# ConvFFN of a diffusion backbone layer: where the up-projection gives back its lead of four pairs

## The chip, the cores and the metric

The kernel runs on one core of one Trainium2 chip. The metric is the device time of one execution, in microseconds; the median of three runs is compared.

## The reference

One layer over 1024 latent tokens of width 1024, with a context prefix of 256: modulated RMSNorm, an input projection that feeds an attention branch and a long-convolution branch, a merge, then a modulated RMSNorm and the ConvFFN, and a final RMSNorm. The change touches the ConvFFN alone:

```python
def dwconv3(u, w, b):
    up = jnp.pad(u, ((0, 0), (1, 1), (0, 0)))
    return up[:, :-2] * w[0] + up[:, 1:-1] * w[1] + up[:, 2:] * w[2] + b

def conv_ffn(h, w_up, b_up, conv_w, conv_b, w_down, b_down):
    u = dwconv3(h @ w_up + b_up, conv_w, conv_b)
    a, g = jnp.split(u, 2, axis=-1)
    return (jax.nn.gelu(a) * g) @ w_down + b_down
```

Here `h` is 1024 x 1024, `w_up` 1024 x 5632 (a and g of 2816 each) and `w_down` 2816 x 1024.

## The kernel before, in words

All products are fp32 in three matmuls (`mm3`, lines 184 to 186): each operand is split into a high part (a cast to fp32r on ScalarE) and a low part (a subtract on VectorE, line 174, "a low" below). High by high, high by low and low by high add up in PSUM.

**The up-projection** goes over 22 pairs j. A pair is 128 columns of a and the same 128 of g, for all 1024 tokens. It is a 2 x 2 block product (halves of the 1024 inputs by halves of the tokens) done with seven products of blocks instead of eight. Each product is 4 x 3 = 12 matmuls of 128 x 512. They are numbered 1 to 7; seq names them (p, j). Their moving operands, sums of the token blocks, stay in SBUF for all pairs: `B1` (tiles m0h and m0l) for 1 and 2, T2, T3, T4, T1 and B22 for 6, 7, 4, 5 and 3. Their weights are made for each pair: the loads of four blocks of `w_up` go into a ring of five `raw` buffers (line 1317), product 6 needs three sums on VectorE (wsum) and product 3 one, and each product one cast (whi) and one low (wlo).

Products 2, 4 and 3 add onto the banks of 1, 7 and 5 after VectorE or ScalarE has read those. In the order of a pair (`behind`, line 1592):

- behind 1: ScalarE copies the bank (c1); behind 6: VectorE's u2 = c1 + bank of 6, and ScalarE's copy ca LOW empties the bank of 1 and 2
- behind 7: VectorE's u3 = u2 + bank of 7; only then may 4 write that bank
- behind 5: cg HIGH = u3 + bank of 5; only then may 3 write that bank
- behind 4: cg LOW = u2 + bank of 7 and 4, then ScalarE's first convolution tap of g (conv ug, line 1556)
- behind 3: ca HIGH = u2 + bank of 5 and 3, then conv ua

Work that can wait goes on a list (`later`, `due`) and is issued one to three products further: VectorE's other two taps of g (taps ug) and of a (taps ua), ScalarE's gelu, VectorE's ug = ua x ug and the store to `act_d`.

**The order** is a list written out by hand (`seq`, lines 1460 to 1469), and the engines' order follows it (`manual_schedule`). Products 1 and 2 of a pair depend on nothing of that pair, so they run four pairs ahead (AHEAD) and stand between 7 and 5, and between 4 and 3, of an earlier pair. Pairs 18 to 21 have no further pair to take them from. In their place stand pieces of the down-projection's first product, (8, 0) to (8, 5), 48 matmuls in all, whose operands are eight blocks of `act_d` and `w_down`, cast and split into the tiles of B1, which are free by then.

While product n runs, `ahead(reach(n))` prepares the weights up to four products further (pieces (8, k) are not counted) and issues loads three products beyond that. In each step stand, in this order: the matmuls, the loads, sums and casts of the preparation, `behind`, the lows of the preparation, and `due`.

**The down-projection** follows: products (9, 4) and (9, 5) still with blocks in the old pools, then units of two blocks from line 1695 on (`fetch_unit`, `prepare_unit`), whose first buffers (ff, raw, rr, bh, bl, ah, al) take the memory of the pools of B1, B22, T1 and the weights.

PSUM holds four banks b1 (for 1 and 2, and for the down-projection's sums X) and four banks b (for 6, 7 and 5).

Of the kernel before, what the change touches and what calls it, by code (L numbers as in the profile page):

```python
# [24 lines left out]
NJ = DFF // P  # L25
# [140 lines left out]
def build(tc, A, out, stop=99):  # L166
# [6 lines left out]
    def sub(out, a, b, eng=V):  # L173
        eng.tensor_tensor(out=out, in0=a, in1=b, op=ALU.subtract)  # L174
# [33 lines left out]
    one = gp.tile([P, 1], F32, name="one")  # L208
# [1233 lines left out]
    def second_tiles(c, late):  # L1442
# [12 lines left out]
        for d, t_ in them:  # L1455
# [4 lines left out]
    AHEAD = 4  # L1460
    second = lambda c: ("T", c)
    seq = [(1, 0), (1, 1), (2, 0), second(0), (2, 1), second(1), (1, 2), second(2), (1, 3), second(3),
           (2, 2), (2, 3)]
    for j in range(NJ):
        more = j + AHEAD < NJ
        early = {18: [(), (8, 0), (8, 1)], 19: [(8, 2), (8, 3)], 20: [(8, 4)], 21: [(8, 5)]}.get(j, [])
        seq += [(6, j), (7, j)] + [(1, j + AHEAD)] * more + early[:1] + [(5, j), (4, j)] + [(2, j + AHEAD)] * more + early[1:] + [(3, j)]
    seq += [(9, 4), (9, 5)]
    seq = [s for s in seq if s]
    prods = [s for s in seq if s[0] != "T"]  # L1470
    raws, sums_, wts, early = {}, {}, {}, {}
    X = [None] * 4
# [8 lines left out]
    def prepare(p, j):  # L1481

        new = lambda: cpool.tile([P, 512], F32, name="wsum", tag="wsum", bufs=3)
        src = None
        if p >= 8:
            if p == 8 and j >= 4:
                return lambda: None
            if p == 8:

                parts_ = [[b_[:, 2 * j + n] for b_ in B1] for n in range(2)]  # L1490
            else:
                parts_ = [[wp.tile([P, 512], F32R, name=t_, tag=t_, bufs=6) for t_ in ("whi", "wlo")] for n in range(2)]
            early[j] = [*parts_[0], *parts_[1]]
            r_ = raws.pop((p, j))
            for d, src in zip(parts_, r_):
                S.copy(out=d[0], in_=src)

            def lows():
                for d, src in zip(parts_, r_):
                    sub(d[1], src, d[0])  # L1500
            return lows
        if p == 6:
            r21, r22, r11 = (raws[6, j, b_] for b_ in (A21, A22, A11))
            s1, s2, s3 = new(), new(), new()
            tt(s1, r21, r22, ALU.add)
            sub(s2, s1, r11)
            sub(s3, r11, r21)
            sums_[j] = s1, s2, s3
            src = s2
        elif p == 7:  # L1510
            src = sums_[j][2]
        elif p == 5:
            src = sums_[j][0]
        elif p == 4:
            src = raws.pop((6, j, A22))
        elif p == 3:
            src = new()
            sub(src, raws.pop((3, j, A12)), sums_.pop(j)[1])
        else:
            src = raws.pop((p, j, A11 if p == 1 else A12))  # L1520
        hi = wp.tile([P, 512], F32R, name="whi", tag="whi", bufs=6)
        S.copy(out=hi, in_=src)
        lo = wp.tile([P, 512], F32R, name="wlo", tag="wlo", bufs=6)
        wts[p, j] = hi, lo
        return lambda: sub(lo, src, hi)
# [45 lines left out]
    def product(p, j):  # L1571
        if p >= 8:
            for i, ks in {(8, 0): ((0, (0,)),), (8, 1): ((0, (1,)),), (8, 2): ((0, (2,)), (1, (0, 1, 2))),
                          (8, 3): ((0, (3,)), (1, (3,))), (8, 4): ((2, (0, 1, 2, 3)),),
                          (8, 5): ((3, (0, 1, 2, 3)),)}.get((p, j), [(i, (j,)) for i in range(4)]):
                for k in ks:
                    if k == 0:
                        X[i] = pa.tile([P, 512], F32, name="b1", tag="b1")
                    down_mm(X[i], i, k, early[k], k == 0, False)
            return  # L1580
        th, tl = {1: [b_[:, 0:4] for b_ in B1], 2: [b_[:, 4:8] for b_ in B1], 3: B22, 4: T4, 5: T1, 6: T2,
                  7: T3}[p]
        key = {2: 1, 4: 7, 3: 5}.get(p, p)
        if key == p:
            banks[key, j] = pa.tile([P, 512], F32, name="b1" if p == 1 else "b", tag="b1" if p == 1 else "b")
        ps = banks[key, j]
        wh, wl = wts.pop((p, j))
        for k in range(4):
            ks = slice(k * P, k * P + P)
            mm3(ps, wh[:, ks], wl[:, ks], th[:, k], tl[:, k], k == 0 and key == p, k == 3, key != p)  # L1590
# [55 lines left out]
    for s in seq:  # L1646
        if s[0] == "T":
            second_tiles(s[1], None)
            continue
        if s == (6, 0):  # L1650
            for pl in (tmp, hf0p, yp1):
                pl.release()
            fw_ = tc.alloc_tile_pool(name="fw_", bufs=1, reuse_waits="tile")
        product(*s)
        n_ += 1
        low = ahead(reach(n_))
        if s[0] == 9:
            continue
        if s == (3, NJ - 1):
            for k in (4, 5):  # L1660
                product(9, k)
        behind(*s)
        for f in low:
            f()
        if s == (3, NJ - 1):
            break
        due()
# [216 lines left out]
```

## Time and profile before

| what | value |
|---|---|
| median of three runs | 2041.69 us (2036.03 to 2044.32) |
| profiled execution: time / span | 2043.09 us / 2041.3 us |
| mean granted TensorE clock | 0.968 |
| busy TensorE / VectorE / ScalarE / GpSimd | 1897.0 / 1569.8 / 975.7 / 436.8 us |
| up-projection, first conv ug of a pair to the last | 1419.94 to 1825.08 us |
| regular pair, 1440 to 1747 us | one every 19.2 us |

The profile is of one execution. Times count from the first instruction. TensorE's weight loads (PEld) run beside its matmuls (PE). Every matmul of 128 x 512 is listed with 0.39 us, but one starts every 0.23 us, so busy times of matmuls overlap; starts are what counts. The value in brackets at a row's end is how long the engine was idle before it and what ended that. The granted clock is 1.00 at 2.4 GHz and 0.50 at 1.2. The program's names lose their numbers in the profile's rows: u2 and u3 are both u, m0h and m0l are B1.

### The profile page before, as it was taken

How to read it: one execution, taken by the hardware profiler on the slowest of the kernel's cores; microseconds unless marked ns; L12 is line 12 of the kernel's file. 1: busy time of each engine (PE TensorE's matmuls, PEld its weight loads, DVE VectorE, ACT ScalarE, POOL GpSimd, SP SyncE). 2: the span in 40 equal slices, each digit the busy share in tenths (PEclk: the TensorE clock that was granted, in tenths of full speed). 3: DMA queues.
4: the chain of work that ended last, by engine and by line, in shares of the span. 5: the costliest groups of instructions: out<-in, count | busy, mean ns of one | idle time of the engine just before them, and what ended most of it. 6: DMA issues, size and time to landing. Idle time of an engine off the chain costs nothing.

```text
span 2041.3 us, 27758 instructions
## 1 busy us (share of the span) xinstructions
PE 1897.0 (93%) x9776; PEld 1572.0 (77%) x9776; DVE 1569.8 (77%) x2634; ACT 975.7 (48%) x1966; POOL 436.8 (21%) x278
## 2 busy tenths in 40 slices
PE   6788899889998998999999999998999999899997
PEld 1576778779888987788888777777888888678885
DVE  6998887697887634577777664789888888878687
ACT  3574544343244345577777332245444444445443
POOL 3453323212122132254432132440000000000000
PEclk8799999999999999999999999999999999899999
DMA  7426523747555441345433884742333323349762
GB/s 258 162 91 206 161 96 126 245 133 249 194 171 154 129 147 57 123 126 161 150 99 49 289 289 138 262 165 73 119 97 115 119 94 118 119 141 346 243 206 100
DMA packets 181131, 322.54 MB, mean 158 GB/s; under 512 B 26955, under 2 KB 65359, under 8 KB 180096
## 3 DMA queue, kind: packets, MB, share of 16 engines
q1 hardware_dynamic: 156256, 287.01, 43.3%
q10 hardware_dynamic: 24736, 33.76, 4.7%
q8 instruction: 77, 1.26, 0.3%
q14 instruction: 62, 0.51, 0.1%
HBM read 245.03 MB, written 75.68 MB: 157 GB/s over the span
## 4 chain that ended last, share of the span: by engine, by line
PE 58%; DVE 23%; DMA 7%; issue 6%; ACT 3%; POOL 2%; SPq 0%; DVEq 0%; ACTq 0%; POOLq 0%
PE mm L185 6%; PE mm L186 6%; PE mm L184 6%; PE b L184 6%; PE b L185 6%; PE b L186 6%; PE tp L1154 3%; DMA wm<-w_mod 2%; PE s L185 2%; PE s L184 2%; PE s L186 2%; POOL wlo L174 2%; PE o L185 2%; PE o L186 2%; PE o L184 2%
## 5 line engine op out<-in xcount | busy, mean ns | idle before, releaser
L174 POOL TENSOR_TENSOR wlo<-raw,whi 128x512 fp32r<-128x512 f32 x138 | 232.5, 1696 | 550.7 <-ACT whi L500 401.5
L184 PE MATMUL mm<-hTh,whi 128*128 128x512 f32 x448 | 179.4, 401 | 1.4 <-ACT sg L983 1.4
L185 PE MATMUL mm<-hTl,whi 128*128 128x512 f32 x448 | 178.5, 399 | 0.7 <-DVE hTl L174 0.7
L186 PE MATMUL mm<-hTh,wlo 128*128 128x512 f32 x448 | 179.0, 399 | 0.0
L1056 DVE TENSOR_REDUCE mx<-s 128x1 f32<-128x512 f32 (+1 forms) x192 | 113.5, 599 | 59.7 <-PE s L186 58.2
L185 PE MATMUL mm<-wlo,hTh 128*128 128x256 f32 x416 | 119.7, 288 | 8.7 <-POOL wlo L174 8.4
L1061 ACT ACTIVATE Pt<-s,mx 128x512 f32<-128x512 f32 (+1 forms) x192 | 116.1, 614 | 20.5 <-DVE mx L1059 19.1
L184 PE MATMUL mm<-whi,hTh 128*128 128x256 f32 x416 | 119.4, 288 | 1.2 <-DVE hf L606 1.2
L186 PE MATMUL mm<-whi,hTl 128*128 128x256 f32 x416 | 119.6, 288 | 0.0
L388 ACT CAST Xh<-X 128x512 fp32r<-128x512 f32 x128 | 78.2, 621 | 86.1 <-DVE X L177 32.4
L174 DVE TENSOR_TENSOR PTl<-tp,PTh 128x512 fp32r<-128x512 f32 x160 | 108.5, 687 | 13.9 <-ACT PTh L1156 10.4
L1156 ACT CAST PTh<-tp 128x512 fp32r<-128x512 f32 x160 | 92.7, 594 | 41.0 <-PE tp L1154 40.6
L186 PE MATMUL b<-bh,al 128*128 128x512 f32 x284 | 110.7, 390 | 0.6 <-DVE al L174 0.6
L184 PE MATMUL b<-bh,ah 128*128 128x512 f32 x284 | 110.7, 390 | 0.5 <-ACT ah L1741 0.5
L185 PE MATMUL b<-bl,ah 128*128 128x512 f32 x284 | 110.6, 390 | 0.0
L500 ACT CAST whi<-raw 128x512 fp32r<-128x512 f32 x110 | 66.7, 618 | 87.8 <-PE mm L185 39.2
L174 DVE TENSOR_TENSOR Xl<-X,Xh 128x512 fp32r<-128x512 f32 x112 | 83.1, 760 | 31.0 <-ACT Xh L388 30.7
L184 PEld LDWEIGHTS mm<-hTh,whi 128*128 128x128 f32 x448 | 85.7, 191 | 16.7 <-ACT sg L983 1.8
L186 PEld LDWEIGHTS mm<-hTh,wlo 128*128 128x128 f32 x448 | 85.7, 191 | 15.8
L185 PEld LDWEIGHTS mm<-hTl,whi 128*128 128x128 f32 x448 | 85.5, 191 | 16.1 <-DVE hTl L174 1.1
L1154 PEld LDWEIGHTS tp<-ident,Pt 128*128 128x128 f32 x640 | 77.8, 141 | 22.9 <-issue 4.0
L1154 PE MATMUL tp<-ident,Pt 128*128 128x128 f32 x640 | 94.4, 274 | 1.0 <-DVE PTl L174 0.8
(396 smaller groups left out, 5833.9 us busy)
## 6 DMA issues: line engine op xcount, KB each, us to landing
raw<-w_up SPq DMA_DIRECT2D x132, 256.0 KB, 2.8
raw<-w_in SPq DMA_DIRECT2D x88, 256.0 KB, 3.3
wm<-w_mod SPq DMA_DIRECT2D x64, 256.0 KB, 4.1
raw<-act_d SPq DMA_DIRECT2D x25, 512.0 KB, 3.2
wd<-w_down SPq DMA_DIRECT2D x44, 256.0 KB, 3.9
ws_d<-wd SPq DMA_DIRECT2D x44, 256.0 KB, 4.5
act_d<-ug SPq DMA_DIRECT2D x44, 256.0 KB, 2.2
ft<-fwd_d SPq DMA_DIRECT2D x28, 384.0 KB, 4.0
```

Source lines behind the costliest of these rows:

```text
L174: eng.tensor_tensor(out=out, in0=a, in1=b, op=ALU.subtract)
L184: T.matmul(o, lh, rh, start=start, stop=False, skip_group_check=more)
L185: T.matmul(o, lh, rl, start=False, stop=False, skip_group_check=more)
L186: last_mm[0] = T.matmul(o, ll, rh, start=False, stop=stop, skip_group_check=more)
L388: S.copy(out=h, in_=X)
L500: S.copy(out=hi, in_=raw)
L1056: V.tensor_reduce(out=mx[:, j:j + 1], in_=s[:, :n], axis=AX.X, op=ALU.max)
L1061: S.activation(out=Pt[:, o:o + n], in_=sps[j][:, :n], func=AF.Exp, bias=mx[:, 3:4], accum_out=sm[:, j:j + 1])
L1154: T.transpose(tp[:, i * P:i * P + P], cur[i][:, kt * P:kt * P + P], ident)
L1156: S.copy(out=th, in_=tp)
```

## The change

Products 1 and 2 of the next pair are left out at three pairs on the way (6, 11 and 16), so the lead falls from four to three, two and one there, and pairs 18 to 20 have products 1 and 2 in their places like the others. All six pieces of the down-projection's first product move to the end: (8, 0) to (8, 3) between 4 and 3 of pair 21, (8, 4) and (8, 5) behind product (3, 21), ahead of (9, 4) and (9, 5). The lows of the early blocks are issued in the preparation, ahead of `behind`, and no longer after it.

```diff
@@ -1461,12 +1461,16 @@
     second = lambda c: ("T", c)
     seq = [(1, 0), (1, 1), (2, 0), second(0), (2, 1), second(1), (1, 2), second(2), (1, 3), second(3),
            (2, 2), (2, 3)]
+    nxt = AHEAD
     for j in range(NJ):
-        more = j + AHEAD < NJ
-        early = {18: [(), (8, 0), (8, 1)], 19: [(8, 2), (8, 3)], 20: [(8, 4)], 21: [(8, 5)]}.get(j, [])
-        seq += [(6, j), (7, j)] + [(1, j + AHEAD)] * more + early[:1] + [(5, j), (4, j)] + [(2, j + AHEAD)] * more + early[1:] + [(3, j)]
+        more = nxt < NJ and j not in (6, 11, 16)
+        one, two = [(1, nxt)] * more, [(2, nxt)] * more
+        nxt += more
+        if j == NJ - 1:
+            one, two = [], [(8, n) for n in range(4)]
+        seq += [(6, j), (7, j)] + one + [(5, j), (4, j)] + two + [(3, j)]
+    seq += [(8, 4), (8, 5)]
     seq += [(9, 4), (9, 5)]
-    seq = [s for s in seq if s]
     prods = [s for s in seq if s[0] != "T"]
@@ -1498,6 +1502,9 @@
             def lows():
                 for d, src in zip(parts_, r_):
                     sub(d[1], src, d[0])
+            if p == 8:
+                lows()
+                return lambda: None
             return lows
@@ -1657,8 +1664,8 @@
         if s[0] == 9:
             continue
         if s == (3, NJ - 1):
-            for k in (4, 5):
-                product(9, k)
+            for x_ in prods[n_:]:
+                product(*x_)
         behind(*s)
```

The order on VectorE in pair 6 before, from u2 (u_15618) over the taps ua of pair 5, u3 (u_15643) and two lows to ug of pair 5 and the sums for pair 7:

```order
L177 TENSOR_TENSOR u_15618<-c_15019,b 128x512
L174 TENSOR_TENSOR wlo<-raw,whi 128x512
L180 SCALAR_TENSOR_TENSOR ua<-ca,vecs,ua 128x1023 x2
L177 TENSOR_TENSOR ua<-ua,edge_ff 128x2
L177 TENSOR_TENSOR u_15643<-u_15618,b 128x512
L174 TENSOR_TENSOR wlo<-raw,whi 128x512
L174 TENSOR_TENSOR wsum<-raw,wsum 128x512
L174 TENSOR_TENSOR wlo<-wsum,whi 128x512
L177 TENSOR_TENSOR ug<-ua,ug 128x1024
L177 TENSOR_TENSOR wsum<-raw 128x512
L174 TENSOR_TENSOR wsum<-wsum,raw 128x512
L174 TENSOR_TENSOR wsum<-raw 128x512
```

The same stretch of VectorE now, from the sum for product 3 that stands ahead of u2 to cg HIGH (u3 is u_15649):

```order
L174 TENSOR_TENSOR wsum<-raw,wsum 128x512
L177 TENSOR_TENSOR u_15618<-c_15019,b 128x512
L174 TENSOR_TENSOR wlo<-wsum,whi 128x512
L180 SCALAR_TENSOR_TENSOR ua<-ca,vecs,ua 128x1023 x2
L177 TENSOR_TENSOR ua<-ua,edge_ff 128x2
L177 TENSOR_TENSOR wsum<-raw 128x512
L174 TENSOR_TENSOR wsum<-wsum,raw 128x512
L174 TENSOR_TENSOR wsum<-raw 128x512
L177 TENSOR_TENSOR u_15649<-u_15618,b 128x512
L174 TENSOR_TENSOR wlo<-wsum,whi 128x512
L177 TENSOR_TENSOR cg<-u_15649,b 128x512
```

The preparation counts in products and a bare pair has fewer of them, so the sums for the next pair stand ahead of u3 now and the sum for product 3 ahead of u2.

The order on VectorE at the start of pair 21 now, from ca HIGH of pair 20 to u3 (u_17991):

```order
L177 TENSOR_TENSOR ca<-u_17769,b 128x512
L174 TENSOR_TENSOR wlo<-raw,whi 128x512
L174 TENSOR_TENSOR m0l<-raw,m0h 128x512 x8
L174 TENSOR_TENSOR wsum<-raw,wsum 128x512
L177 TENSOR_TENSOR u_17959<-c_17816,b 128x512
L174 TENSOR_TENSOR wlo<-wsum,whi 128x512
L180 SCALAR_TENSOR_TENSOR ua<-ca,vecs,ua 128x1023 x2
L177 TENSOR_TENSOR ua<-ua,edge_ff 128x2
L177 TENSOR_TENSOR u_17991<-u_17959,b 128x512
```

All eight lows of the early blocks stand there in one piece, ahead of the sum for product 3 and of u2; before, they stood in pair 18 (four behind u2, two behind cg LOW) and pair 19 (two).

## Rows read from the trace of the kernel before

**Rows 1.** The stretch 1440 to 1747 (busy us and count by engine, clock, DMA).

```profile
core 0: us, PE busy (x) PEld busy (x) DVE busy (x) ACT busy (x) POOL busy (x), PEclk, DMA share, GB/s
1440.00:1747.00 307.00, 307.00 (x1349) 251.96 (x1348) 262.04 (x368) 134.73 (x192) 0.00 (x0) 1.00 0.34 110
```

**Rows 2.** Waits of VectorE and of TensorE's weight loads, 1440 to 1747 (total, times, longest).

```profile
DVE wlo L174 <- ACT whi L1522: 42.1, 48, 1.2
PEld b L184 <- ACT ca L1604: 3.0, 11, 0.3
```

**Rows 3.** Timeline of ScalarE: conv ug of pairs 16 and 17 (start, us, [idle before]).

```profile
1728.02 1.24 ACT L1556 ACTIVATE ug<-cg,cbias_ff,vecs 128x1024 f32<-128x1024 f32 x1 [1.18 <-DVE cg L177]
...
1747.22 1.25 ACT L1556 ACTIVATE ug<-cg,cbias_ff,vecs 128x1024 f32<-128x1024 f32 x1 [1.18 <-DVE cg L177]
```

**Rows 4.** Timeline of VectorE, pair 18 without the lead's products.

```profile
1752.32 0.68 DVE L177 TENSOR_TENSOR ca<-u,b 128x512 f32<-128x512 f32 x1
1752.92 0.68 DVE L174 TENSOR_TENSOR wlo<-raw,whi 128x512 fp32r<-128x512 f32 x1
1756.28 0.69 DVE L174 TENSOR_TENSOR wsum<-raw,wsum 128x512 f32<-128x512 f32 x1 [2.68 <-DMA raw<-w_up]
...
1757.49 2.49 DVE L174 TENSOR_TENSOR m0l<-raw,m0h 128x512 fp32r<-128x512 f32 x4
1759.90 0.69 DVE L174 TENSOR_TENSOR wlo<-wsum,whi 128x512 fp32r<-128x512 f32 x1
1760.50 2.60 DVE L180 SCALAR_TENSOR_TENSOR ua<-ca,vecs,ua 128x1023 f32<-128x1023 f32 x2
...
1765.15 0.68 DVE L177 TENSOR_TENSOR u<-u,b 128x512 f32<-128x512 f32 x1
...
1771.47 0.69 DVE L177 TENSOR_TENSOR cg<-u,b 128x512 f32<-128x512 f32 x1 [2.70 <-PE b L186]
```

**Rows 5.** Timeline of TensorE, pair 18; the last row is pair 21.

```profile
1757.85 0.39 PE L186 MATMUL b<-m1l,wlo 128*128 128x512 f32 x1
1765.97 0.77 PE L184 MATMUL b<-T4h,whi 128*128 128x512 f32 x1 [7.73 <-DVE u L177]
...
1772.30 0.40 PE L184 MATMUL b<-m0h 128*128 128x512 f32 x1
...
1815.84 0.50 PE L184 MATMUL b<-m0h 128*128 128x512 f32 x1 [0.45 <-ACT ca L1604]
```

**Rows 6.** Timeline of ScalarE: casts of four early blocks, pair 18.

```profile
1754.25 2.17 ACT L1496 CAST m0h<-raw 128x512 fp32r<-128x512 f32 x4
```

**Rows 7.** Timeline of TensorE: three other idles of some 3 us.

```profile
537.03 0.58 PE L184 MATMUL zp<-Xh,ft 128*128 128x256 f32 x1 [3.10 <-ACT Xh L388]
...
834.77 0.50 PE L184 MATMUL o<-PTh,v 128*128 128x512 f32 x1 [2.74 <-ACT PTh L1156]
...
1302.49 0.39 PE L1202 MATMUL tr<-ah,ones 128*1 128x512 f32 x1 [3.10 <-ACT ah L1198]
```

**Rows 8.** Windows behind those idles, columns as in rows 1.

```profile
537.00:541.00 4.00, 3.97 (x18) 3.97 (x19) 3.21 (x8) 1.14 (x2) 2.76 (x1) 0.50 0.01 2
836.50:840.50 4.00, 4.00 (x16) 3.29 (x15) 1.86 (x3) 1.47 (x4) 0.19 (x1) 0.57 0.98 345
1302.50:1306.50 4.00, 3.78 (x16) 2.81 (x17) 4.00 (x4) 0.62 (x1) 2.27 (x2) 1.00 0.92 294
```

**Rows 9.** Timeline of SP's queue, ScalarE and TensorE: the down-projection starts.

```profile
1822.59 0.40 SPq L1695 DMA_DIRECT2D ff<-act_d  x1
1827.07 0.38 SPq L1695 DMA_DIRECT2D ff<-w_down  x1
...
1830.93 1.05 ACT L1740 CAST bh<-ff 128x1024 fp32r<-128x1024 f32 x1 [1.83 <-DMA ff<-w_down]
...
1832.98 0.50 PE L184 MATMUL b<-bh,ah 128*128 128x512 f32 x1 [0.50 <-ACT ah L1741]
```

**Rows 10.** Tile raw, 1745 to 1775: its loads from issue to landing.

```profile
DMA to landing us min/median/max: 2.7/2.9/3.1
```

## The prediction

> **What bounds the kernel now.** I read four views of the up-projection stage, in this order. First the busy table of the regular stretch, pairs 2 to 17: TensorE is busy 307.00 of 307 us, VectorE 262.04 [rows 1]. That alone says TensorE is the limit. Second, who waits for whom there: VectorE's only wait is for ScalarE's casts, 42.1 us in 48 waits, and the only one on TensorE's side is 3.0 us in 11 weight loads, for ScalarE's copy that empties a bank [rows 2]; ScalarE's waits are all for VectorE. Neither of the two waits for TensorE. Third, the period: one pair takes 1747.22 - 1728.02 = 19.20 us [rows 3]. VectorE's work is 262.04 / 16 pairs = 16.4 us and its waits 42.1 / 16 = 2.6 us, 19.0 together, so the closed loop of VectorE and ScalarE fills the period. TensorE's 84 matmuls at 307.00 / 1349 = 0.2276 us are 19.1 us [rows 1]. So **two engines are level, and it is VectorE and ScalarE that set the pace**: a pair with fewer matmuls gets shorter only by what VectorE does less in it.
>
> Fourth, the first pair without the lead's products, pair 18, is a sample of what the change makes three times. Its product 4 starts at 1765.97 after 7.73 us of idle TensorE, released by VectorE's u3 (u<-u,b in the rows) [rows 5]. Product 4 adds onto the bank of product 7, so u3 must have read that bank first. VectorE is late because it waits 2.68 us for a raw load, then runs four lows of the early products, then taps and three sums ahead of u3 [rows 4].
>
> **The change, part by part.** Matmuls, casts, lows and transfers are the same in number, so I add up what TensorE waits; its work cancels. All is against the profiled execution, 2043.09 us around a span of 2041.3, which is 1.40 above the median of the three runs, 2041.69.
>
> (a) *Pairs 6, 11 and 16 lose products 1 and 2* (24 matmuls, 24 x 0.2276 = 5.46 us of cover each). Take pair 18's rows and remove what a bare pair in the middle doesn't have. The raw wait, 2.68 us, goes: that load waited for a slot of the five raw buffers, which the early products' blocks held, and in pair 6 the slot comes from product 2 of the pair before, long released. The four lows go, 1759.90 - 1757.49 = 2.41 us (2.49 with the last one's drain) [rows 4]. Then u3 starts at 1765.15 - 2.68 - 2.41 = 1760.06; some 0.15 us come back, where the cast of the sum that the raw wait hid is now waited for. u3 ends 0.68 us later at 1760.9 and product 4 follows 0.14 us behind, as it did from 1765.83 to 1765.97: 1761.0 [rows 4, 5]. TensorE had finished product 5 at 1757.85 + 0.39 = 1758.24 [rows 5]. Idle: 2.8 us, three times **8.4 us**. Bounds for each: 0 if u3 were covered; 5.5 if the raw wait stays. I take 2.8, because the raw buffers' order speaks against the wait and nothing shortens the sums.
>
> (b) *Pair 18 gets its products back.* Its 7.73 us of idle go, and so does the half clock behind it: from 1765.97 to 1772.30 fifteen matmuls started in 6.33 us instead of 15 x 0.2276 = 3.41, 2.9 us lost. A wait of 0.45 us in pair 21 goes too [rows 5]. Together **-11.1 us**.
>
> (c) *Pair 21 now holds all eight early blocks.* Count from ca HIGH of pair 20 (1752.32 in the sample) [rows 4]. ScalarE's casts can start at 1.9 (1754.25), 0.54 each [rows 6]. VectorE's first low is at 2.6; four blocks are there. The fifth block's load waits for the low of pair 21's product 4, done at 1.3; the sixth's for the first low (ends 3.3), and so on, because raw has five buffers; a load lands 2.9 us after its issue (2.7 to 3.1) [rows 10]. So the fifth low runs at about 5.0, the sixth at 6.8, the eighth ends at 8.6, and the load of product 3, asked for after the fourth low (5.1), is there at 8.0. Then the sum 8.6, u2 9.2, a cast's wait and the low to 10.6, taps 10.6 to 13.3 (2.60 and the edge), u3 to 14.0, product 4 at 14.1. TensorE is through with product 5 at 1758.24 - 1752.32 = 5.9. Idle 8.2 us, and a half clock behind it as behind the 7.73: 2.9. Together **+11.1 us**. Bounds: 7.0 us of idle if no load were late, 10.2 if each late load took a microsecond more.
>
> (d) *The start of the down-projection.* Its first loads go into memory of m0 and m1. Before, the activation's load left at 1822.59 and the weights' at 1827.07, at the end of product (3, 21); the weights' cast began at 1830.93, and TensorE waited 0.50 us for the cast behind it [rows 9]. Now products (8, 4) and (8, 5) read m0 behind (3, 21), and both loads leave together at the end of (8, 5), two products from the end, where (3, 21) stood before. The weights' load leaves one issue later, some 0.4 us (0.38 for one), and shares the queues with the other. I take **+0.9 us**, between 0.4 and 4.5 (1827.07 - 1822.59, if the activation's lead were needed).
>
> (e) *Where I cost nothing.* The regular pairs keep 19.2 us with a shorter lead, since order and work per pair are the same. The early lows issued inside the preparation stand ahead of the last pair's u2 as they would behind it. Taps ug of pair 21 move ahead of the down-projection's preparation, 2.7 us less for VectorE there, where TensorE had no other wait.
>
> (f) *The clock behind the three new idles.* Granted 1.00 is 2.4 GHz and 0.50 is 1.2. Idles of this length in this trace: 3.10 us before 1302.49, granted clock 1.00 after it; 3.10 before 537.03, then 0.50; 2.74 before 834.77, then 0.57 from 836.5 to 840.5 [rows 7, 8]. Two of three lost the clock. A loss costs 4.0 x (1 - 0.57) = 1.7 us [rows 8] to 2.9 (pair 18), and all of it lies on the path, as VectorE waits for product 4 there (2.70 us at 1771.47) [rows 4]. Bounds: none, or three at 2.9. I take one at the middle, **+2.3 us**; two is nearly as likely.
>
> Sum: 8.4 - 11.1 + 11.1 + 0.9 + 2.3 = +11.6 us, so 2041.69 + 11.6 = **2053.3 us**, slower by 0.57%. A measurement of this kernel tells about 0.5% from no change, 10.2 us.
>
> **Rivals.**
> 1. *The bare pairs are covered.* If u3 came by 1758.2 in a bare pair, the 8.4 and the 2.3 vanish: +0.9 us, 2042.6, not slower. For it: one pair every five could draw on slack. Against it: seven VectorE operations (some 7 us) stand between the end of the pair before and u3 [rows 4], and VectorE has no slack to draw on [rows 2]. It decides as soon as u3 ends before product 5 does. 0.13.
> 2. *TensorE paces everything.* The bare pairs are covered, pair 21's blocks come early enough (another 11.1 less), and the wait for a bank goes: four b1 buffers make (1, j + 4) wait for pair j under a lead of four, 3.0 us in all [rows 2], and a shorter lead ends that. 2042.6 - 11.1 - 3.0 = 2028.5. For it: 307.00 of 307 busy [rows 1]. Against it: VectorE never waits for TensorE [rows 2], and the five raw buffers. The Trainium skill (Perfetto Trace Analysis, Optimization Strategy) says that a gap which keeps coming back on the engine that should be saturated can mean too few buffers; by that rule the 3.0 us would be a gain, and rows 2 disagree. 0.07.
> 3. *The clock stays.* The forecast without its last term: 9.3 us, 2051.0, inside 0.5%. For it: the idle before 1302.49 [rows 7, 8]. 0.21.
> 4. *The clock goes all three times.* 9.3 + 3 x 2.3 = 16.2 us, 2057.9. For it: two of the three idles; against it, the third [rows 7, 8]. The Trainium skill (TensorE: Matmul & The Clock Gate, Part 1: The HAM clock gate) says that the throttled state is the default and activity releases it; by that rule each idle would be followed by the lower clock, and the idle before 1302.49 does not agree. 0.12.
> 5. *The transition is starved.* The down-projection's loads all follow (8, 5), and its units arrive late: (d) at 4.5 instead of 0.9: 2056.9, or 2061 with two or three losses of the clock. For it: the cast there waited 1.83 us for its load already [rows 9]. Against it: TensorE still has two products behind the first load. 0.12.
>
> That the change doesn't do what it says can be left out: the products stand on TensorE in the order of the table, which is written out by hand.
>
> **How the numbers follow.** The forecast, one or two losses of the clock, has 0.35; with them it spans 2051.5 to 2056 or so. From rival 1's 2042.6 to rival 5's 2061, 2042 to 2061 leaves out rival 2 and the far ends of 1 and 5, some 0.15 to 0.2. Faster by over 0.5%: rival 2, 0.07. Within 0.5%: rivals 1 and 3, 0.34. Slower: 0.35 + 0.12 + 0.12 = 0.59.
>
> **What would show it.** Right: three idles of about 2.8 us before product 4 of pairs 6, 11 and 16, released by u3; periods of about 17.5 and 18 us for such a pair and the next; pair 18 regular at 19.2; one idle of about 8 us before product 4 of pair 21, with VectorE waiting for raw among the eight lows. Wrong: bare pairs without an idle, or with one over 4 us that ends on a load; a pair 21 that TensorE passes without stopping; regular pairs that change their 19.2 us once the lead is shorter; an idle over 3 us before the first product of the down-projection.

## The result and the profile after

| | before | after |
|---|---|---|
| median of 6 runs each | 2041.54 us (2036.03 to 2046.57) | 2056.92 us (2050.46 to 2061.84) |
| ratio, 95% interval | | 1.0077 (1.0063 to 1.0090) |
| profiled execution: own time, span | 2043.09, 2041.3 us | 2050.46, 2048.7 us |
| from conv ug of pair 0 to the first product of the down-projection | 413.04 us | 424.73 us |

The changed kernel is 0.77% slower, 15.4 us (12.9 to 18.4 by the interval). 2053.3 was forecast, with a range of 2042 to 2061: the result is inside the range, but the 11.6 us of the forecast are less than the interval allows. The profiled executions differ by only 7.4 us, because work ahead of the stage ended 5.88 us earlier in that of after (conv ug of pair 0 at 1414.06 instead of 1419.94). So I compare the stage with itself, in the table's last row: +11.69 us up to the down-projection, and some 1.7 us behind it, below. There is one profile of each kernel, so what a row says holds for one execution, and only the medians tell what is usual.

First the waits of the stage after, 1434 to 1817 (total, times, longest).

```profile
DVE wlo L174 <- ACT whi L1529: 41.7, 49, 1.2
...
PE b L184 <- DVE u L177: 18.1, 4, 9.1
```

VectorE still waits for casts as in [rows 2]. New is the second row: TensorE waits four times for VectorE's u, 18.1 us in all. Each of the four is in its timeline, with the start of the down-projection behind them:

```profile
1524.70 0.47 PE L184 MATMUL b<-T4h,whi 128*128 128x512 f32 x1 [2.60 <-DVE u L177]
...
1617.89 0.47 PE L184 MATMUL b<-T4h,whi 128*128 128x512 f32 x1 [3.19 <-DVE u L177]
...
1712.73 0.47 PE L184 MATMUL b<-T4h,whi 128*128 128x512 f32 x1 [3.21 <-DVE u L177]
...
1813.50 0.77 PE L184 MATMUL b<-T4h,whi 128*128 128x512 f32 x1 [9.10 <-DVE u L177]
...
1838.79 0.50 PE L184 MATMUL b<-bh,ah 128*128 128x512 f32 x1 [1.80 <-ACT ah L1748]
```

They are product 4 of pairs 6, 11, 16 and 21, each behind u3, as pair 18 was before [rows 5]. The windows behind these five, columns as in rows 1, show what the clock did:

```profile
1524.70:1528.70 4.00, 4.00 (x18) 3.33 (x19) 3.79 (x6) 1.65 (x4) 0.00 (x0) 1.00 0.57 167
1617.90:1621.90 4.00, 4.00 (x11) 3.15 (x12) 2.78 (x4) 1.36 (x3) 0.00 (x0) 0.59 0.49 167
1712.70:1716.70 4.00, 3.97 (x12) 3.22 (x13) 2.83 (x4) 1.41 (x3) 0.00 (x0) 0.68 0.50 164
1813.50:1817.50 4.00, 4.00 (x11) 3.20 (x12) 3.99 (x6) 1.44 (x3) 0.00 (x0) 0.62 0.01 4
1838.80:1845.00 6.20, 5.57 (x16) 4.13 (x17) 5.76 (x6) 3.03 (x4) 0.00 (x0) 0.72 1.05 388
```

TensorE kept full speed behind the first, and fell to half (1.2 GHz) for part of the window behind the other four. Behind pair 16 the window ends before the clock is back: the next 4 us still have 0.89. At the start of the down-projection that is 6.2 x (1 - 0.72) = 1.7 us which the kernel before did not lose: there 1833.0 to 1839.2 had a granted clock of 1.00.

ScalarE's conv ug gives the periods, with pair 6 bare:

```profile
1510.86 1.25 ACT L1563 ACTIVATE ug<-cg,cbias_ff,vecs 128x1024 f32<-128x1024 f32 x1 [1.18 <-DVE cg L177]
...
1528.42 1.24 ACT L1563 ACTIVATE ug<-cg,cbias_ff,vecs 128x1024 f32<-128x1024 f32 x1 [2.35 <-DVE cg L177]
...
1546.46 1.25 ACT L1563 ACTIVATE ug<-cg,cbias_ff,vecs 128x1024 f32<-128x1024 f32 x1 [1.18 <-DVE cg L177]
```

A bare pair and the next took 17.56 + 18.04 = 35.60 us, against 38.40 for two regular ones, although 24 matmuls (5.46 us) had gone. Around pairs 11 and 16 it was 37.23 and 37.26. The other pairs from 2 to 20 kept 19.20, pair 18 among them (pair 1 took 20.0 in both kernels); pair 21 took 24.93 against the 24.97 of pair 18 before.

VectorE shows why u3 is late. In bare pair 11 the taps of the pair before and the next pair's three sums stand between u2 and u3 (1617.07):

```profile
1610.96 0.68 DVE L177 TENSOR_TENSOR u<-c,b 128x512 f32<-128x512 f32 x1
...
1612.42 2.60 DVE L180 SCALAR_TENSOR_TENSOR ua<-ca,vecs,ua 128x1023 f32<-128x1023 f32 x2
...
1615.13 0.69 DVE L177 TENSOR_TENSOR wsum<-raw 128x512 f32<-128x512 f32 x1
1615.85 0.69 DVE L174 TENSOR_TENSOR wsum<-wsum,raw 128x512 f32<-128x512 f32 x1
1616.46 0.68 DVE L174 TENSOR_TENSOR wsum<-raw 128x512 f32<-128x512 f32 x1
1617.07 0.68 DVE L177 TENSOR_TENSOR u<-u,b 128x512 f32<-128x512 f32 x1
```

In pair 21 all eight lows of the early blocks stand ahead of u2, and the last three wait for casts of blocks whose loads are late:

```profile
1798.87 0.68 DVE L177 TENSOR_TENSOR ca<-u,b 128x512 f32<-128x512 f32 x1
...
1801.43 3.10 DVE L174 TENSOR_TENSOR m0l<-raw,m0h 128x512 fp32r<-128x512 f32 x5 [1.28 <-ACT m0h L1500]
1805.51 0.69 DVE L174 TENSOR_TENSOR m0l<-raw,m0h 128x512 fp32r<-128x512 f32 x1 [0.98 <-ACT m0h L1500]
1806.55 1.46 DVE L174 TENSOR_TENSOR m0l<-raw,m0h 128x512 fp32r<-128x512 f32 x2 [0.35 <-ACT m0h L1500]
...
1808.53 0.68 DVE L177 TENSOR_TENSOR u<-c,b 128x512 f32<-128x512 f32 x1
...
1809.96 2.60 DVE L180 SCALAR_TENSOR_TENSOR ua<-ca,vecs,ua 128x1023 f32<-128x1023 f32 x2
...
1812.67 0.68 DVE L177 TENSOR_TENSOR u<-u,b 128x512 f32<-128x512 f32 x1
```

From ca HIGH to u3 these are 13.80 us; the forecast's count had 13.3 (14.0 less u3's own 0.7). And at the start of the down-projection both loads leave together, behind product (8, 5). Before, that of the activation left 4.48 us ahead of the other [rows 9]:

```profile
1831.58 0.37 SPq L1702 DMA_DIRECT2D ff<-act_d  x1
1831.99 0.47 SPq L1702 DMA_DIRECT2D ff<-w_down  x1
```

### The profile page after: what moved, and what is told of

Same layout as the page of the kernel before. It is cut to its first block, busy times and chain, and to the rows that moved or that the text cites. A ratio compares the mean times of both kernels' runs of the same rounds, so it can differ in the third digit from the quotient of the medians.

```text
span 2048.7 us, 27776 instructions
## 1 busy us (share of the span) xinstructions
PE 1895.6 (93%) x9776; PEld 1574.3 (77%) x9776; DVE 1567.3 (77%) x2634; ACT 976.0 (48%) x1966; POOL 435.2 (21%) x278
## 4 chain that ended last, share of the span: by engine, by line
PE 63%; DVE 20%; DMA 6%; issue 5%; ACT 3%; POOL 2%; SPq 0%; ACTq 0%; DVEq 0%; POOLq 0%
PE b L184 7%; PE b L186 7%; PE b L185 7%; PE mm L186 6%; PE mm L185 6%; PE mm L184 6%; PE tp L1154 3%; PE s L185 2%; PE s L184 2%; PE s L186 2%; PE o L185 2%; PE o L186 2%; PE o L184 2%; DMA wm<-w_mod 2%; POOL wlo L174 1%
## 5 line engine op out<-in xcount | busy, mean ns | idle before, releaser
L174 DVE TENSOR_TENSOR PTl<-tp,PTh 128x512 fp32r<-128x512 f32 x160 | 108.3, 686 | 14.0 <-ACT PTh L1156 10.4
```

## The experiments

The theory: on VectorE's fixed order everything that stands ahead of u3 is paid by TensorE as soon as no product of the lead covers it. Its parts are the sums in a bare pair, the early lows in pair 21, the clock behind long idles, and the loop of VectorE and ScalarE that leaves nothing in hand. Each ratio is against runs of the kernel before on the same chip; the difference is between the two medians there, and is clear of noise only where the interval leaves out 1; the last column is the stage of one execution, as in the first table.

| run | edit | median us | ratio, 95% interval | difference us | stage us |
|---|---|---|---|---|---|
| e1 | after, early blocks spread | 2051.96 | 1.0049 (1.0037 to 1.0062) | +10.9 | 417.63 |
| e2 | after, u3 first | 2051.76 | 1.0051 (1.0033 to 1.0069) | +10.7 | 420.74 |
| e3 | e1 and e2 | 2042.57 | 1.0005 (0.9995 to 1.0015) | +1.5 | 413.02 |
| e8 | e3, six pieces inside pair 21 | 2039.85 | 0.9993 (0.9980 to 1.0006) | -0.3 | 411.93 |
| e9 | after, idles filled | 2051.18 | 1.0048 (1.0031 to 1.0065) | +9.6 | 423.04 |
| e12 | after, taps first | 2045.11 | 1.0027 (1.0015 to 1.0039) | +5.0 | 414.99 |
| e11 | after, all orders | 2026.38 | 0.9936 (0.9913 to 0.9959) | -15.2 | 400.59 |
| e4 | before, u3 first | 2039.10 | 0.9986 (0.9977 to 0.9994) | -2.0 | 410.68 |
| e5 | before, a low twice | 2041.77 | 1.0014 (0.9998 to 1.0030) | +1.6 | 413.54 |
| e6 | before, taps first | 2035.80 | 0.9984 (0.9968 to 1.0000) | -4.3 | 408.07 |
| e7 | before, two sums on GpSimd | 2039.51 | 0.9996 (0.9984 to 1.0007) | -0.6 | 410.04 |
| e10 | e4 and e6 | 2033.73 | 0.9961 (0.9949 to 0.9973) | -7.8 | 405.57 |

**e2, u3 ahead of the sums.** The edit, on the changed kernel:

```
         product(*s)
         n_ += 1
+        if s[0] == 7:
+            behind(*s)
         low = ahead(reach(n_))
...
-        behind(*s)
+        if s[0] != 7:
+            behind(*s)
```

> The changed kernel, but u3 is issued on VectorE ahead of the preparation that follows product 7, so in a bare pair the next pair's three sums (1.93 us) stand behind u3. Regular pairs keep their order. Theory (VectorE's order sets the idle of a bare pair): the idles before product 4 of pairs 6, 11 and 16 fall from 2.60, 3.19 and 3.21 us by about 1.9 each to 0.7 to 1.3, and the two half clocks behind them (2 us each) go: 5.8 + 4 = some 10 us less than the changed kernel, about 2047. Rival A (VectorE and ScalarE as a closed loop are a fixed amount of work per pair): the sums are late instead, the next pair's product 6 waits for its cast, and the period of the two pairs together stays 35.6 us; change under 2 us. Rival B (the clock is no matter of the idle's length): the idles shrink, the clock is still lost, 5 to 6 us less.

TensorE's timeline of e2, pairs 6, 11 and 21:

```profile
1526.72 0.47 PE L184 MATMUL b<-T4h,whi 128*128 128x512 f32 x1 [0.66 <-DVE u L177]
...
1530.10 0.47 PE L184 MATMUL b<-m1h,whi 128*128 128x512 f32 x1 [0.42 <-ACT whi L1529]
...
1619.33 0.47 PE L184 MATMUL b<-T4h,whi 128*128 128x512 f32 x1 [1.89 <-DVE u L177]
...
1813.00 0.76 PE L184 MATMUL b<-T4h,whi 128*128 128x512 f32 x1 [10.34 <-DVE u L177]
```

The three idles fell to 0.66, 1.89 and 1.91 us and no bare pair lost the clock (granted 1.00 behind all three). But the gain was about half of the 10 us expected. The rows show four things that took the rest. The idles of pairs 11 and 16 fell by 1.3 and not by 1.9 (why stays open); the sum of product 3, now late, made TensorE wait 0.4 us more in each (the row at 1530.10); the half clocks had cost 1.7 us each and not 2; and part of what TensorE gained it lost again in pair 21, whose idle grew from 9.10 to 10.34, with VectorE's last early lows waiting 2.1 us for their casts instead of 1.3. A bare pair and the next took 35.00 us instead of 35.60, 37.23 and 37.26: 5.1 us from the three. Rival A was not the case, but there was something of it, since neither VectorE nor ScalarE had less to do: in pair 6, where no clock was lost, the idle fell by 1.94 us, the new wait took 0.42, and the period with the next fell by only 0.60.

**e1, the early blocks one at a time.** `reach` counts them, so that they are prepared as the products go by:

```
-            c += prods[n][0] != 8
+            c += prods[n] not in [(8, 4), (8, 5)]
```

> The changed kernel, but the four early blocks of the down-projection count in the preparation's look-ahead, so they are prepared one per product over pair 21 and not all eight casts and lows ahead of u2. Theory (VectorE's order sets when u3 comes): only two lows stand ahead of u2 instead of eight, u3 comes some 6 us earlier, the idle before product 4 of pair 21 goes from 9.10 us to 2 or 3, and the half clock behind it (1.5 us) may stay: 6 to 8.5 us less than the changed kernel, about 2049 to 2051. Rival A (the five raw buffers and the loads set it): the lows come as late as before, the idle only moves behind product 4, to an early product or product 3, and the total changes by less than 2 us. Rival B (the cost of the change is in the three bare pairs and the clock): pair 21 is worth under 3 us.

Product 4 of pair 21 in e1:

```profile
1816.61 0.68 PE L184 MATMUL b<-T4h,whi 128*128 128x512 f32 x1 [3.61 <-DVE u L177]
```

The idle of pair 21 fell from 9.10 to 3.61 us, and half clock stayed behind it (0.57 over 4 us). Nothing moved behind product 4, so the raw loads (rival A) were not the limit. By the medians the gain was 15.4 - 10.9 = 4.5 us, less than the 6 to 8.5 expected, but each of the two differences is known only to some 2.5 us either way. In the stage it is 424.73 - 417.63 = 7.1 us, of which 5.5 is this idle, longer than the 2 to 3 us expected, and 1.6 comes from the clock, which pair 16 kept in this profile. Behind the idles of 3.20 us (pair 11) and 3.22 us (pair 16) the windows of e1 are

```profile
1628.10:1632.10 4.00, 3.98 (x11) 3.21 (x12) 2.81 (x4) 1.39 (x3) 0.00 (x0) 0.61 0.50 163
1723.00:1727.00 4.00, 4.00 (x18) 3.31 (x19) 3.77 (x6) 1.62 (x4) 0.00 (x0) 1.00 0.51 171
```

the same idle with and without the loss.

**e3, both.**

> Both edits together on the changed kernel. Theory: the gains add, 16 to 18 us less than the changed kernel, about 2039 to 2041, level with or just under the kernel before (2041.5); in pair 21 u3 also stands ahead of two more lows, so its idle is 1 to 2 us. Rival: a loop of VectorE and ScalarE that is full in every pair takes part of it back: 2045 to 2049.

2042.57 us, +1.5 on the kernel before, which the interval does not tell from none: 13.9 us less than the changed kernel, where 16 to 18 were expected. In the stage 11.7 us of the 11.69 came back, more than 7.1 + 4.0 by a little. Against e1 u3 now also stands ahead of two early lows that ran before it there, and pair 21's idle is 0.6 us shorter, though not the 1 to 2 us expected:

```profile
1804.50 0.47 PE L184 MATMUL b<-T4h,whi 128*128 128x512 f32 x1 [3.03 <-DVE u L177]
```

So two pieces of VectorE's order account for the loss up to the down-projection. What is left of the difference, if it is one, fits the half clock behind the start (granted 0.72 over 6.2 us in e3 too).

**e8, six pieces inside pair 21.** Added to e3:

```
-            one, two = [], [(8, n) for n in range(4)]
+            one, two = [], [(8, n) for n in range(6)]
...
-    seq += [(8, 4), (8, 5)]
```

> Both edits of before on the changed kernel (early blocks spread over pair 21, u3 first), and products (8, 4) and (8, 5) inside pair 21, ahead of product (3, 21), where the kernel before had (8, 5), instead of behind it. Theory (the down-projection's first loads wait for the last reader of the memory of m0 and so leave too late behind (8, 5)): the idle before the first product of the down-projection falls from 1.74 to about 0.5 us as in the kernel before, and the half clock behind it (0.72 over 6 us, 1.7 us) goes: 3 us less than with both edits alone (2042.6), 2039.5. Rival (the loads are not what that product waits for; what changed is VectorE's and ScalarE's order there): the idle stays 1.7, no change.

TensorE at the start of the down-projection, and the window behind it:

```profile
1826.17 0.50 PE L184 MATMUL b<-bh,ah 128*128 128x512 f32 x1 [0.53 <-ACT ah L1750]
```

```profile
1826.20:1832.40 6.20, 5.56 (x23) 4.31 (x24) 5.76 (x6) 3.04 (x4) 0.00 (x0) 1.00 1.05 387
```

Idle 0.53 instead of e3's 1.74 and clock 1.00 instead of 0.72, as expected: 1.2 and 1.7 us, together the 3 us forecast for this. In the medians, each against the kernel before on its own chip, e8 is 1.8 us under e3 (-0.3 and +1.5), and the two intervals overlap. The load of the activation left 2.72 us ahead of that of the weights again (1817.51 and 1820.23).

**e9, the idles filled.** Matmuls into a bank nobody reads, in the idle of the bare pairs; the result stays as it is:

```
+        if p == 5 and j in (6, 11, 16):
+            spare = pa.tile([P, 512], F32, name="b1", tag="b1")
+            for k in range(3):
+                ks = slice(k * P, k * P + P)
+                mm3(spare, wh[:, ks], wl[:, ks], th[:, k], tl[:, k], k == 0, k == 2)
```

> The changed kernel, with nine matmuls more behind product 5 of pairs 6, 11 and 16, into a bank that nobody reads (9 x 0.2276 = 2.05 us, inside the idle of 2.60 to 3.21 us; the result is unchanged). They cost no time if u3 is what product 4 waits for; they only shorten the idle to 0.5 to 1.2 us. Theory (what followed two of the three idles at half clock is lost because of the idle): periods of 37.2 us for pairs 11 and 16 with the next become 35.6, 1.6 less each, 3 to 4 us less than the changed kernel, 2053 to 2054. Rival A (clock and idle are unrelated here): half clocks as before, no change. Rival B (product 4 waits for TensorE's own order, not u3): 3 x 2.05 = 6 us slower.

TensorE in pairs 11, 16 and 21 and at the start of the down-projection, and two windows:

```profile
1619.94 0.47 PE L184 MATMUL b<-T4h,whi 128*128 128x512 f32 x1 [1.18 <-DVE u L177]
...
1713.20 0.47 PE L184 MATMUL b<-T4h,whi 128*128 128x512 f32 x1 [1.18 <-DVE u L177]
...
1812.88 0.77 PE L184 MATMUL b<-T4h,whi 128*128 128x512 f32 x1 [9.63 <-DVE u L177]
...
1839.15 0.49 PE L184 MATMUL b<-bh,ah 128*128 128x512 f32 x1 [1.81 <-ACT ah L1753]
```

```profile
1619.90:1623.90 4.00, 3.96 (x17) 3.30 (x18) 3.74 (x6) 1.60 (x4) 0.00 (x0) 1.00 0.50 166
...
1839.10:1845.30 6.20, 5.51 (x23) 4.25 (x24) 5.77 (x6) 3.04 (x4) 0.00 (x0) 1.00 1.05 387
```

With 27 more matmuls the medians are 5.8 us under those of the changed kernel (15.4 - 9.6), where 3 to 4 were expected. Pairs 11 and 16 with the next fell to 35.65 us, 1.6 us each, which is the price of the clock where it was lost, and no bare pair lost it. The profile shows less in all than the medians. Pair 21 took 26.38 us instead of 24.93, with a longer idle (9.63) and a longer half clock behind it (0.50 over 4 us), so the stage is only 1.7 us shorter. The last window was not expected: the start's idle is as in the changed kernel, 1.81 us, but its clock stayed at 1.00, which is another 1.7 us. Why it stayed there, the rows don't tell.

Two pairs that kept the clock in one execution would prove little, since e1 has one that kept it without a filler. The bare pairs of all the profiles on the changed kernel's order say more: 17 idles of 0.48 to 2.61 us kept the clock (changed kernel, e1, e2, e3, e8, e9, e12), and of four of 3.19 to 3.22 us three lost it. So in these pairs the clock went with the idle, and Rival A is not the case.

**e4, u3 first in the kernel before.** The edit of e2.

> The kernel before, with u3 issued ahead of the preparation behind product 7. Only pairs 18 to 20 change, where no lead's product stands between. Theory: in pair 18 the three sums (1.93 us) and the two lows of an early block move behind u3, the idle of 7.73 us before product 4 falls by 1.9 to 4.4, the half clock behind it stays or goes (2.9): 2 to 7 us less than the kernel before, 2035 to 2039.6. Rival (the late load paces pair 18): the idle moves to product 3 or to pair 19's product 6, change under 1 us.

2.0 us less, at the low end: pair 18's idle fell from 7.73 to 5.75 us, about the three sums' 1.93, and the half clock stayed (0.55 over 6 us).

**e5, a low computed twice.** On the kernel before:

```
-        return lambda: sub(lo, src, hi)
+        def low_():
+            sub(lo, src, hi)
+            if p == 5:
+                sub(lo, src, hi)
+        return low_
```

> The kernel before, with the low of product 5's weights computed twice on VectorE in every pair (0.6 us more of VectorE's work a pair, nothing more for the others; the result is unchanged). Theory (the closed loop of VectorE and ScalarE sets the regular period): 19.2 becomes 19.8 us, 22 x 0.6 = 13 us slower, 2054. Rival (TensorE sets the period and VectorE's 2.6 us of waits a pair are slack): the period stays 19.2, under 1 us slower in the regular pairs, at most 3 in all.

The regular period stayed at 19.20 us, so this one spoke against the theory as it was put. The trace shows where the 0.6 us went. The second low came just ahead of u2 and of the low of a cast for which VectorE had waited 0.68 us in every pair; that wait vanished. VectorE's waits for casts in e5, 1642 to 1700, three pairs; in the kernel before the same row reads 7.9 us in 9:

```profile
DVE wlo L174 <- ACT whi L1522: 5.9, 6, 1.2
```

So VectorE's busy time is not the pace, and there is slack at that place. What the pace is, e6 tells.

**e6, taps ahead of the lows.** On the kernel before:

```
         behind(*s)
+        if s != (3, NJ - 1):
+            due()
         for f in low:
             f()
         if s == (3, NJ - 1):
             break
-        due()
```

> The kernel before, with the work that is due (taps, products) issued on VectorE ahead of the lows of the same step instead of behind them, so the casts that the lows wait for have time; no engine's work changes. Theory (closed loop): of the 2.6 us a pair that VectorE waits for casts, 1.2 to 2.6 go, the period falls from 19.20 to TensorE's own 19.1 and TensorE becomes the limit: 2 us less in the regular pairs, up to 2 more in pair 18: 2037.5 to 2039.5. Rival A (TensorE sets 19.2 already): period stays 19.20, under 1 us. Rival B (the taps come too early and wait for their activation): VectorE's waits stay at 2.6 us or grow, equal or slower.

ScalarE's conv ug of pairs 16 and 17 and VectorE's waits, 1460 to 1740:

```profile
1720.61 1.24 ACT L1556 ACTIVATE ug<-cg,cbias_ff,vecs 128x1024 f32<-128x1024 f32 x1 [1.48 <-DVE cg L177]
...
1739.65 1.25 ACT L1556 ACTIVATE ug<-cg,cbias_ff,vecs 128x1024 f32<-128x1024 f32 x1 [1.48 <-DVE cg L177]
```

```profile
DVE u L177 <- PE b L186: 21.4, 15, 1.4
```

The period is 19.04 us, and now VectorE waits for TensorE in every pair, which it never did before [rows 2]. With the same work on every engine, only the order of VectorE made the difference: 19.20 was the closed loop, by a margin of 0.16 over TensorE's own 19.04. The medians differ by 4.3 us, more than the 2 to 4 expected, but with an interval that just reaches 1; the period is the surer evidence. Together with e5 it says what the loop is not: a sum of VectorE's work and waits. It must be a chain through certain casts and the operations behind them. Which ones was not followed, only that 0.6 us of work put into a wait cost nothing.

**e7, two sums on GpSimd.** On the kernel before:

```
-            sub(s3, r11, r21)
+            sub(s3, r11, r21, G)
...
-            sub(src, raws.pop((3, j, A12)), sums_.pop(j)[1])
+            sub(src, raws.pop((3, j, A12)), sums_.pop(j)[1], G)
```

> The kernel before, with two of the four sums of each pair (the third one and that of product 3) on GpSimd, which is idle in this stage, instead of VectorE: 1.2 us less a pair for VectorE, 2 x 1.3 us for GpSimd. Theory (closed loop): the period falls to TensorE's own 19.1, 2 us less; pair 18's idle of 7.73 falls by 0.6. 2038 to 2040. Rival A (TensorE sets the period): under 1 us. Rival B (a sum on GpSimd comes later than on VectorE, ScalarE's cast of it and the low behind it wait): period 19.5 or more, 7 us slower or more.

The regular period fell to 19.05 us and the stage by 3.0 us in this profile, but the medians show no difference that stands (0.9984 to 1.0007). What was expected of VectorE's 1.2 us a pair did not come. GpSimd's third sum, and VectorE's ug and first sum beside it, in one pair:

```profile
1661.15 2.21 POOL L174 TENSOR_TENSOR wsum<-raw 128x512 f32<-128x512 f32 x1 [11.61 <-DVE wlo L174]
```

```profile
1660.99 1.22 DVE L177 TENSOR_TENSOR ug<-ua,ug 128x1024 f32<-128x1024 f32 x1
1662.13 1.78 DVE L177 TENSOR_TENSOR wsum<-raw 128x512 f32<-128x512 f32 x1
```

VectorE's sum took 1.78 instead of 0.69 us, and over 15 pairs VectorE was busy for 245.75 us with 316 instructions, where before it was busy for 245.83 us with 346: the 30 sums that left saved it nothing. Its waits for casts fell from 39.6 to 36.0 us in the same pairs, and it had none for TensorE; whether the loop or TensorE sets 19.05 us here stays open. Pair 1 became 0.67 us longer, pair 19 1.42 us longer and pair 18 1.35 us shorter.

**e12, taps first in the changed kernel.** The edit of e6 alone.

> The changed kernel with the taps ahead of the lows and nothing else (early blocks in one go, u3 behind the sums, (8, 4) and (8, 5) behind pair 21, as the change has them). Theory (VectorE late by its order): regular pairs 19.04, 3 us less; in a bare pair u2 now waits for TensorE, so from the end of product 6 u2, taps, a low, three sums and u3 are 0.6 + 2.8 + 0.6 + 1.9 + 0.7 = 6.6 us against 5.5 us of products 7 and 5: idles of 1.1 to 1.4 us instead of 2.60, 3.19 and 3.21, and no half clock behind them, 5 us plus 3 to 4 less. Pair 21 keeps its 9 to 10 us of idle. Together 11 to 12 us less than the changed kernel, 2044 to 2046. Rival A (only u3's own place counts in a bare pair): the idles stay 2.6 us or more, 3 us less, 2053. Rival B (the spread of the early blocks counts for nothing once VectorE has slack): pair 21's idle falls below 4 us as well, 2038 or less.

TensorE in pairs 11 and 21:

```profile
1616.28 0.47 PE L184 MATMUL b<-T4h,whi 128*128 128x512 f32 x1 [1.27 <-DVE u L177]
...
1804.60 0.77 PE L184 MATMUL b<-T4h,whi 128*128 128x512 f32 x1 [6.99 <-DVE u L177]
```

2045.11 us, in the range expected; against the kernel before on its own chip that is 10.4 us less than the changed kernel (15.4 - 5.0), for 11 to 12. The three bare pairs idle 1.27 us each, all alike, at a granted clock of 1.00; they no longer grow from the first to the second, which fits TensorE pacing now and having no lead to gain. Pair 21 kept most of its idle, 6.99 us.

**e10 and e11, the orders together.** e10 is the kernel before with the edits of e2 and e6; e11 is the changed kernel with the edits of e1, e2, e6 and e8, and with the early lows in the list that follows `behind`, as the kernel before has them:

```
-            if p == 8:
-                lows()
-                return lambda: None
             return lows
```

> The kernel before with both orders of VectorE: u3 ahead of the preparation behind product 7, and the due taps ahead of the lows. Theory: the gains are in different places (pair 18's idle; the 0.16 us of every pair) and add, 2.0 + 3.3 to 4.3 = 5.3 to 6.3 us less than the kernel before, 2034 to 2036; regular pairs 19.04. Rival: pair 18 is held by its late load whatever the order (5.75 and 5.93 us with one order each), so the second order finds nothing there: 2036 to 2037.

> The changed kernel with all edits: early blocks spread over pair 21 with their lows behind u2, u3 first, (8, 4) and (8, 5) inside pair 21, taps ahead of the lows. Theory (VectorE's order, and nothing else, is what the change paid for): regular pairs 19.04, 22 x 0.16 = 3.5 us less than 2039.85, the bare pairs' idles under 1.9 us and that of pair 21 under 3 us: 2033 to 2036, the same as the kernel before with both orders or below. Rival (the raw loads hold pair 21 as they hold pair 18 in the kernel before): pair 21 keeps 3 us or more, 2036 to 2038.

e10 gave 2033.73 us: the two gains add, to a little more than their sum (2.0 + 4.3 against 7.8), and pair 18's idle fell to 3.53 us, so its late load had not been all of it. e11 gave 2026.38 us, 15.2 us under the kernel before and better than the 2033 to 2036 expected. Against e10, the kernel before with the same orders, it is 7.4 us less in the medians, with intervals that overlap, and 5.0 us less in the stage. From conv ug of pair 1 to that of pair 21 the window of e11 and its row of waits, 1436 to 1815, are

```profile
1434.56:1798.87 364.31, 364.29 (x1604) 300.54 (x1603) 324.17 (x453) 163.91 (x234) 0.00 (x0) 1.00 0.34 112
```

```profile
DVE u L177 <- PE b L186: 20.2, 17, 1.4
```

TensorE has not one idle in it, bare pairs and pair 21 included, and its clock stays at 1.00 throughout. The expectation had left idles of up to 1.9 us in the bare pairs and up to 3 in pair 21. The idea of the change holds, then: with the lead given back on the way and all early pieces in one pair TensorE need not stop at all, if VectorE has u3 ready. Whether in pair 21 it was the taps or the lows behind u2 and u3 that took the last 3.02 us of e8's idle, e11 does not tell, since it has both.

## Why the prediction was right

The sign and the mechanism were right, idle for idle; the time was 3.8 us too low. Point by point, in the prediction's letters:

- (a) The three idles of 2.8 us were 2.60, 3.19 and 3.21, released by u3 behind the sums: 9.0 us for 8.4. They grew because TensorE at 19.04 us a pair runs ahead of a loop at 19.20 once it need not wait for a bank: product 4 of pairs 7 to 10 started every 19.04 us (1541.10 to 1598.22), and the conv ug of the same pairs came every 19.20. In e12, where TensorE paces, the idle is 1.27 three times.
- (b) Pair 18 is regular at 19.20, as forecast, and its 7.73 us, with the half clock behind them, are gone.
- (c) Pair 21's idle was 9.10 us for 8.2, for the reason given: eight lows, the last of them on late loads. The half clock behind it cost 4.0 x (1 - 0.62) = 1.5 us and not 2.9. Together 10.6 for 11.1, and that this is so near is luck: one part was too small and the other too large. e1 and e3 show the lows to be the cause.
- (d) The start idled 1.80 us instead of 0.50, 1.3 us for 0.9, and e8 takes it back. **What failed is in this step**: the half clock behind that idle, 1.7 us, was not in the sum. I had looked for it behind idles of about 3 us only.
- (e) Regular pairs stayed at 19.20 us with the shorter lead, though TensorE's weight loads no longer waited for ScalarE's ca: 3.0 us before [rows 2], and no such wait from 1434 to 1817 after. So the bank was not what held the pair at 19.20, and the 3.0 us that the second rival hoped for from it were no gain.
- (f) Two bare pairs lost the clock where I took one, at 1.7 us each over the 8 us behind the idle: 3.4 us for 2.3. Idles of 3.20 and 3.22 us with and without the loss, in e1, say that a count of past cases was all that one had.

By the profile the sum is 9.0 - 11.1 + 10.6 + 1.3 + 1.7 + 3.4 = 14.9 us. From the stage's own times it is 11.69 + 1.7 = 13.4. So not every idle lengthened the kernel: what TensorE idles because it had run ahead costs nothing. In e1, with the clock kept both times, pair 6 and the next took 35.63 us with an idle of 2.61, and pair 16 and the next 35.62 with one of 3.22. The medians differ by 15.4 (12.9 to 18.4), so up to 2 us have no row, which is inside the interval.

The median, 2056.9, lies nearer to the fourth rival (2057.9) and the fifth (2056.9) than to the forecast, but neither is what the rows show: the clock went in two bare pairs of three, and the start cost 1.3 us of idle and 1.7 of clock, against the 4.5 of idle that the fifth had. Of the other rivals, the covered bare pairs and the pacing TensorE were not there in the changed kernel, and e6, e12 and e11 show what kept them away: VectorE's order, not its work. e11 came out at 2026.4 us, near the 2028.5 of the second rival, with bare pairs covered and pair 21 passed as it said; the gain from the bank that it also named was not one, see (e), and the 0.16 us of every regular pair came in its place. Against the forecast's claim on the pace one correction stands: "a pair with fewer matmuls gets shorter only by what VectorE does less in it" was too strong, since e5 added work to VectorE and the pair stayed as it was; so was the sum of VectorE's work and waits that it rested on.

## What to carry to other kernels

Work that runs ahead on the busiest engine is cover for the other engines' order; before it is taken out of a stage, find the operation that the busiest engine will then wait for, look at what stands ahead of it on its own engine, and move that first. Here a few lines of order, nearly all VectorE's, with no less work, were worth 30 us on the changed kernel, twice what the change had cost. An engine can be 100% busy by the profile while a loop of two others sets the period: here the two differ by under 1%, 19.04 and 19.20 us. The test is to reorder one of the others: if it then waits for the busy engine and the period falls, the loop had set the pace.

## What the runs showed of the hardware

- Behind the same idle the granted clock stayed or fell: 3.20 us in a bare pair fell and 3.22 did not (e1); 1.80 us at the start of the down-projection fell (changed kernel) and 1.81 did not (e9). The six idles of 1.87 to 1.92 us in bare pairs of e2, e3 and e8 kept it, while at the start those of 1.66 to 1.88 us in e1, e2, e3 and e12 lost it. The length of the idle alone does not tell, but within the bare pairs it did count: 17 idles of 0.48 to 2.61 us kept the clock, three of four of 3.19 to 3.22 lost it.
- With matmuls into an unread bank in the idles of the bare pairs the clock stayed at 1.00 in all three, and the medians fell by 5.8 us with 27 matmuls more (e9); the profile shows 3.4 of it, half of that at the start of the down-projection, where nothing was filled.
- Sums of 128 x 512 that ran on GpSimd and VectorE at once took longer on both: 2.21 us where GpSimd's other sum took 1.30, and 1.78 instead of 0.69 on VectorE (e7). GpSimd's sum started during VectorE's ug and ended 1.15 us behind it, and VectorE's sum ended 0.55 us behind GpSimd's. That fits each waiting for the other's operation to end; no run was made on this alone.
